# Layer 2 of a hybrid decoder step: when the evictions, reloads and the decode chain are issued

## The chip, the cores and the metric

One core of a Trainium2 chip runs the whole kernel. The metric is the device time of one execution in microseconds (us); the kernel before takes 1352.14 us (median of 3 runs, 1352.06 to 1353.18). The engines are PE (TensorE), DVE (VectorE), ACT (ScalarE) and POOL (GpSimd), each with its own queue of instructions that it works off in order; SP (SyncE) issues most transfers from a queue of its own.

## The reference, cut to what matters

Two layers run over a prompt of 1024 tokens and 8 single decode tokens, with model width 1024, in float32. Layer 1 is retention and is not touched. Layer 2 is sliding-window attention with 16 query heads of 64 in 2 groups and a window of 128:

```python
h = rmsnorm(x, g_norm)
q, k, v, gate = jnp.split(h @ w_in, [SWA_Q, SWA_Q + SWA_KV, SWA_Q + 2 * SWA_KV], axis=-1)
q, k = rmsnorm(q, q_gain), rmsnorm(k, k_gain)          # per head
# prompt: query block i of 128 reads key blocks i-1 and i
scores = q @ k.T * SWA_HD ** -0.5 - slope * dist        # banded, ALiBi
p = sink_softmax(scores, sinks)                         # one more column, dropped afterwards
o = (p @ v) * jax.nn.silu(gate)
return x + o @ w_out
# decode: the same over cache_k, cache_v (128 positions) and the new token
```

## The kernel before

Every operand of a big matmul is held as a high part and a low part, `A_hi` and `A_lo`, weights `wh` and `wl`. One product is three matmuls of 128 rows: high by high (L1134), high by low (L1135), low by high (L1136). `proj` writes these three for one k of eight.

Layer 2 begins near 900 us with keys and values. Then the q and gate projections run for 8 pairs of heads (`pair_proj`). A pair has three column groups of the tokens, `TG`: 0 to 384, 384 to 768, 768 to 1032 (the last 8 are the decode tokens), and so 6 tiles of 24 matmuls: q0, q1, q2, g0, g1, g2 (for the last pair g0 stands before q2 and g1 before g2). The tiles take turns on two PSUM banks (`pj`). A q tile is evicted by `q_hi` (ACT: a square for the norm, two high parts) and a tick later by `q_lo` (DVE: two low parts); a gate tile by `g_x` (DVE), `g_t` (ACT) and `g_m` (POOL, two products). `ms_mm` and `ms_ev` find the norm factors `rq`, with a power function on POOL (L118).

The attention has 64 units, one for a pair and a block of 128 tokens. A loop over frames m works on four units at once; in frame m it does `att_s` and `att_b` for unit m+3 (scores on PE, bias and maximum on DVE), `att_e` (exponentials, ACT) and `att_n` (DVE reciprocal, POOL multiplication, line L1680) for unit m+2, `att_x`, `att_ph`, `att_pl` (PE transposes into `tr`, ACT and DVE split) for unit m+1, `att_o` for unit m (product with the values into the single bank `o`, L1710 and L1708), and `att_c` for unit m-1 (two ACT copies at 0.5, two DVE operations L1732, one POOL product with the gate).

A frame has three thirds. Each ends with `work(0.865)`, which lets the projections put about 0.865 us of matmuls into the PE queue, and with `tick()`, which issues what `later(d, ...)` had put off by d ticks. Within layer 2's frames the order of the code is the order in each engine's queue, so a wait of one instruction holds all behind it on that engine.

Other work goes into the frames as jobs (`Job`, `loads`, `parts`). A job loads a raw tile `wr` (two buffers) and then runs its parts, at most two a frame. A part is the conversion of 512 columns of a weight (ACT high, POOL low, L1105 and L1106), a transposition of the key cache, or a reload of the gated attention output. That output is stored to DRAM (`oscr`) per pair and column group, since `A_hi` and `A_lo` still hold the gate's input. `reload_jobs(ti)` brings k = 0 to 6 of a column group back in four pieces, when all gate tiles of that group are done (`g7`): ACT writes `A_hi`, DVE writes `A_lo` (L1485). k = 7 comes straight from `att_st`.

When the projections are used up, `work` takes tiles of the output projection (`so_all`) instead. `start` runs 7 of 8 k-steps into a bank once the whole column group is reloaded (`rready`), `finish` does the last one, adds the residual on DVE (L1878) and has the tile before it transposed and stored (`so_y`). The column groups are gone through one after the other, six row tiles (`ft`) each, and tiles 6 and 7 at the end.

The decode tokens are a chain of five steps after the last frame: `dec_r` (a norm factor on DVE with a POOL power, L1754 to L1758), `dec_scores` (PE, L1770), `dec_soft` (DVE and ACT), `dec_pt` (PE transposes), `dec_o` (PE, L1812). Between them the tail does a reload part and fills PE with output tiles. At that point the order by hand ends (`sk.close()`), and the framework sets the order of all but PE.

Of the kernel before, what the change touches and what calls it, by code (L numbers as in the profile page):

```python
# [73 lines left out]
def _trunk(ctx, tc, nc, a):  # L74
# [1363 lines left out]
    rready = [False] * 3  # L1438

    class Job:  # L1440
        def __init__(self, load, parts, can_load=None, can=None):
            self.load, self.parts = load, list(parts)
            self.can_load, self.can, self.at = can_load, can, None

# [6 lines left out]
    def cache_job():  # L1451
        def load():
            kcT["c"] = wp.tile([128, 8, 128], F32, tag="wr", bufs=2, name="wr")
            nc.sync.dma_start(out=kcT["c"], in_=cache_k[0].rearrange("b s g d -> s b (g d)"))
            kcT["t"] = acc[:, 0:1024].rearrange("p (b s) -> p b s", b=8)

        def part(hf):
            pt = trp.tile([128, 512], F32, name="tr")
            for i in range(4):
                tr(pt[:, i * 128:i * 128 + 128], kcT["c"][:, 4 * hf + i, :], ident)  # L1460
            nc.scalar.activation(acc[:, 512 * hf:512 * hf + 512], pt, AF.Copy)

# [5 lines left out]
        jobs.append(Job(load, [lambda: part(0), lambda: part(1), new]))  # L1468

    def reload_jobs(ti):  # L1470

        t0, t1 = TG[ti]
        t1 = min(t1, NP)
        n = t1 - t0
        for k in range(0, 7, 2):
            m = min(2, 7 - k)
            g = {}

            def load(k=k, m=m, g=g):
                g["t"] = wp.tile([128, 2, n], F32, tag="wr", bufs=2, name="wr")  # L1480
                nc.sync.dma_start(out=g["t"][:, :m, :], in_=oscr[k:k + m, :, t0:t1].rearrange("k p t -> p k t"))

            def part(k=k, m=m, g=g):
                nc.scalar.activation(A_hi[:, k:k + m, t0:t1], g["t"][:, :m, :], AF.Copy)
                nc.vector.tensor_tensor(A_lo[:, k:k + m, t0:t1], g["t"][:, :m, :], A_hif[:, k:k + m, t0:t1],  # L1485
                                        ALU.subtract)
# [29 lines left out]
    def pair_proj(p):  # L1516
# [42 lines left out]
        def ms_ev(ti, pm):  # L1559
            t0, t1 = TG[ti]  # L1560
            nch = (min(t1, NP) - t0) // 128
            c0 = t0 // 128
            ee = e9[:, c0:c0 + nch].unsqueeze(2).broadcast_to([128, nch, 2])
            rq = atp.tile([128, 3, 2], F32, name="rq", bufs=4)
            rqn = rq[:, :nch, :]
            rqf = rq.rearrange("p c i -> p (c i)")[:, :2 * nch]

            nc.vector.scalar_tensor_tensor(rqn, pm[:, :2 * nch].rearrange("p (c i) -> p c i", i=2), 1.0 / HD, ee,
                                           ALU.mult, ALU.add)
            rsq(rqf, rqf, 2 * nch)  # L1570
            if ti == 2:
# [18 lines left out]
        def g_m(ti, gx, gt):  # L1590
            n = TG[ti][1] - TG[ti][0]
            nc.gpsimd.tensor_tensor(gt[:, :n], gt[:, :n], gx[:, :n], ALU.mult)  # L1592
# [6 lines left out]
        mms = {(1, 3): 0, (2, 3): 1, (4 if p == 7 else 3, 3): 2}  # L1599
        for step, (kind, ti) in enumerate(order):  # L1600
# [11 lines left out]
            for k in range(8):  # L1612
# [3 lines left out]
                if k == 7:  # L1616
                    (q_hi if isq else g_x)(ti, ps[:, :n])
# [22 lines left out]
    def bias_tab(h):  # L1640

        ndp[h] = atp.tile([128, 256], F32, name="ndp", bufs=3)
        nc.gpsimd.tensor_scalar(ndp[h], negd, SLOPE[h], None, ALU.mult)

# [106 lines left out]
    def dec_r():  # L1751
# [6 lines left out]
        nc.vector.tensor_tensor(r16, r16, rr, ALU.mult)  # L1758
        ddec = dd["ddec"] = atp.tile([16, 129], F32, tag="s", name="ddec", bufs=6)
        nc.sync.dma_start(out=ddec, in_=a["c2"][0:16, c2w() - 129:])  # L1760
        vc = dd["v"] = wp.tile([128, 8, 128], F32, tag="wr", bufs=2, name="wr")
# [17 lines left out]
    def dec_soft():  # L1779
        S16 = dd["S"]  # L1780
        nc.vector.tensor_tensor(S16, S16, dd["ddec"].unsqueeze(1).broadcast_to([16, 8, 129]), ALU.add)
        nc.vector.tensor_reduce(m16, S16, mybir.AxisListType.X, ALU.max)
        nc.vector.tensor_scalar(m16, m16, skc, None, ALU.max)
# [4 lines left out]
        nc.vector.tensor_reduce(t16, S16, mybir.AxisListType.X, ALU.add)  # L1788
        nc.vector.tensor_tensor(t16, t16, e16, ALU.add)
        nc.vector.reciprocal(t16, t16)  # L1790
        nc.vector.tensor_tensor(S16, S16, t16.unsqueeze(2).broadcast_to([16, 8, 129]), ALU.mult)
# [43 lines left out]
    def so_y(ft, ti, yt):  # L1835
        t0, t1 = TG[ti]
        npr = min(t1, NP) - t0
        nch = npr // 128
# [3 lines left out]
        if ti == 2:  # L1842
            tr(pt[:8, 256:384], yt[:, 256:264], ident)
        yo = atp.tile([128, 384], F32, tag="ot", name="yo", bufs=2)
# [7 lines left out]
    def so_all():  # L1852
        order = [(ft, ti) for ti in range(3) for ft in range(6)] + [(ft, ti) for ft in (6, 7) for ti in range(3)]
        early = []

        def start(ft, ti):
            t0, t1 = TG[ti]
            n = t1 - t0
            while so_slot(ft // 2) is None or not rready[ti] or (ti == 2 and "done" not in dd):
# [7 lines left out]
            for k in range(7):  # L1867
                proj(ps[:, :n], slot, ft % 2, t0, t1, first=(k == 0), last=False, ks=[k])
# [3 lines left out]
        def finish():  # L1872
# [4 lines left out]
            yt = io("sq", 2)  # L1877
            nc.vector.tensor_tensor(yt[:, :n], ps[:, :n], xr[:, :n], ALU.add)  # L1878
            if pend_y:
                so_y(*pend_y.pop(0))  # L1880
            pend_y.append((ft, ti, yt))
# [10 lines left out]
        while pend_y:  # L1892
            so_y(*pend_y.pop(0))
# [98 lines left out]
    for m in range(-L, NU + 1):  # L1992
        frame[0] = m
        w = W if m >= 0 else 1.15
        new, e, x, o, c = unit(m + L), unit(m + L - 1), unit(m + 1), unit(m), unit(m - 1)
# [14 lines left out]
        if e:  # L2010
            att_n(e)
        if x:
# [14 lines left out]
        parts(*((2, 1) if m >= 50 else (1, 2)))  # L2027
        loads()
        work(w)
        tick()  # L2030
    while post:
        tick()
    sk.close()
    steps = [dec_r, dec_scores, dec_soft, dec_pt, dec_o]
    while jobs or steps:
        frame[0] += 2
        loads()
        parts(1, 0)
        fill(out, 1.0)
        if steps and not (steps[0] is dec_r and len(jobs) > 1):  # L2040
            steps.pop(0)()
            fill(out, 1.5)
# [39 lines left out]
```

## Time and profile before

| | |
|---|---|
| median of 3 runs | 1352.14 us (1352.06 to 1353.18) |
| profiled execution | 1350.48 us, of which the span from first to last instruction is 1348.7 |
| PE busy, weight loads busy | 1300.1 us (96%), 1237.7 us (92%) |
| DVE, ACT, POOL busy | 746.6, 667.9, 819.9 us |
| PE busy from 900 us on | 426.2 of 448.7 us |
| mean granted clock of PE | 0.989 |

Busy times overlap, since the engines work side by side. PE is busy nearly always, so only two things can be gained around it: time in which it waits, and time in which its clock is below full. The profile names a waiting instruction by its line, and what released it. An idle engine other than PE costs nothing by itself.

### The profile page before, as it was taken

How to read it: one execution, taken by the hardware profiler on the slowest of the kernel's cores; microseconds unless marked ns; L12 is line 12 of the kernel's file. 1: busy time of each engine (PE TensorE's matmuls, PEld its weight loads, DVE VectorE, ACT ScalarE, POOL GpSimd, SP SyncE). 2: the span in 40 equal slices, each digit the busy share in tenths (PEclk: the TensorE clock that was granted, in tenths of full speed). 3: DMA queues.
4: the chain of work that ended last, by engine and by line, in shares of the span. 5: the costliest groups of instructions: out<-in, count | busy, mean ns of one | idle time of the engine just before them, and what ended most of it. 6: DMA issues, size and time to landing. Idle time of an engine off the chain costs nothing. (4 is left out here: it accounts for less than half of the span.)

```text
span 1348.7 us, 25969 instructions
## 1 busy us (share of the span) xinstructions
PE 1300.1 (96%) x9421; PEld 1237.7 (92%) x9421; DVE 746.6 (55%) x1507; ACT 667.9 (50%) x1692; POOL 819.9 (61%) x958
## 2 busy tenths in 40 slices
PE   6999999999999999899989999999999999997998
PEld 6999999999999999787877889999999999996998
DVE  6943655666565653577762212326777677776511
ACT  5532555555565653576750112245666767665321
POOL 6753555647556664598976663545778877766110
PEclk9999999999999999999998999999999999997999
DMA  6314767577676852656545444443022111013532
GB/s 221 104 55 134 224 200 239 164 236 227 185 227 196 242 159 69 209 177 211 165 164 176 142 154 135 129 117 98 23 63 64 42 48 42 23 53 112 156 89 80
DMA packets 193859, 187.18 MB, mean 139 GB/s; under 512 B 12756, under 2 KB 173580, under 8 KB 193716
## 3 DMA queue, kind: packets, MB, share of 16 engines
q1 hardware_dynamic: 160336, 153.19, 36.8%
q10 hardware_dynamic: 33396, 32.34, 7.7%
q8 instruction: 74, 1.21, 0.4%
q14 instruction: 53, 0.43, 0.1%
HBM read 129.11 MB, written 57.41 MB: 138 GB/s over the span
## 5 line engine op out<-in xcount | busy, mean ns | idle before, releaser
L340 PE MATMUL b<-xh,woh 128*128 128x258 f32 x784 | 222.2, 283 | 0.0
L342 PE MATMUL b<-xh,wol 128*128 128x258 f32 x784 | 221.7, 283 | 0.0
L341 PE MATMUL b<-xl,woh 128*128 128x258 f32 x784 | 221.4, 282 | 0.0
L1134 PE MATMUL pj<-A_hi,wh 128*128 128x384 f32 (+1 forms) x512 | 174.3, 340 | 0.0
L1135 PE MATMUL pj<-A_lo,wh 128*128 128x384 f32 (+1 forms) x512 | 165.6, 323 | 0.1
L1136 PE MATMUL pj<-A_hi,wl 128*128 128x384 f32 (+1 forms) x512 | 165.2, 323 | 0.0
L340 PEld LDWEIGHTS b<-xh,woh 128*128 128x128 f32 x784 | 148.1, 189 | 1.2
L341 PEld LDWEIGHTS b<-xl,woh 128*128 128x128 f32 x784 | 148.7, 190 | 0.0
L342 PEld LDWEIGHTS b<-xh,wol 128*128 128x128 f32 x784 | 148.0, 189 | 0.0
L1124 POOL TENSOR_TENSOR wl<-wr,wh 128x1024 fp32r<-128x1024 f32 (+1 forms) x40 | 88.5, 2222 | 87.4 <-ACT wh L1121 50.6
L334 PE MATMUL b<-wol,xh 128*128 128x256 f32 x448 | 126.0, 281 | 1.2 <-DVE wol L224 1.2
L333 PE MATMUL b<-woh,xh 128*128 128x256 f32 x448 | 125.8, 281 | 0.0
L335 PE MATMUL b<-woh,xl 128*128 128x256 f32 x448 | 125.7, 281 | 0.0
L282 POOL TENSOR_TENSOR yl<-yd,yh 128x256 fp32r<-128x256 f32 x64 | 56.4, 882 | 80.9 <-PE od L289 39.0
L1135 PEld LDWEIGHTS pj<-A_lo,wh 128*128 128x128 f32 x512 | 97.7, 191 | 0.4 <-DVE A_lo L1747 0.4
L224 POOL TENSOR_TENSOR wol<-raw,woh 128x512 fp32r<-128x512 f32 x52 | 68.8, 1331 | 48.1 <-ACT woh L219 47.2
L1134 PEld LDWEIGHTS pj<-A_hi,wh 128*128 128x128 f32 x512 | 97.5, 190 | 0.4
L1136 PEld LDWEIGHTS pj<-A_hi,wl 128*128 128x128 f32 x512 | 97.2, 190 | 0.0
L1680 POOL TENSOR_TENSOR s<-s,sm 128x512 f32<-128x512 f32 x64 | 66.4, 1038 | 31.9 <-DVE sm L1679 30.1
L334 PEld LDWEIGHTS b<-wol,xh 128*128 128x128 f32 x448 | 84.3, 188 | 1.4 <-DVE wol L224 1.4
L333 PEld LDWEIGHTS b<-woh,xh 128*128 128x128 f32 x448 | 84.3, 188 | 0.7
L335 PEld LDWEIGHTS b<-woh,xl 128*128 128x128 f32 x448 | 84.3, 188 | 0.0
(386 smaller groups left out, 3868.6 us busy)
## 6 DMA issues: line engine op xcount, KB each, us to landing
raw<-in_w_in_ret_dram ACTq DMA_DIRECT2D x44, 512.0 KB
st<-in_state_ret_dram SPq DMA_DIRECT2D x64, 256.0 KB
out_dram<-st SPq DMA_DIRECT2D x64, 256.0 KB
wr<-in_w_out_ret_dram SPq DMA_DIRECT2D x32, 512.0 KB
wr<-in_w_in_swa_dram SPq DMA_DIRECT2D x18, 512.0 KB
vb<-vscr SPq DMA_DIRECT2D x64, 128.0 KB
evp<-qks SPq DMA_DIRECT2D x32, 256.0 KB
evw<-gsc SPq DMA_DIRECT2D x32, 256.0 KB
```

The source lines that it names most:

```text
L224: eng.tensor_tensor(lo, src_of(s, name, sub), hi.bitcast(F32), SUB)
L333: mm(dst, xh, wh, start=a and i == 0, stop=False, skip_group_check=True)
L334: mm(dst, xh, wl, start=False, stop=False, skip_group_check=True)
L335: mm(dst, xl, wh, start=False, stop=z, skip_group_check=True)
L340: mm(dst, wh, xh, start=a, stop=False, **sg)
L341: mm(dst, wh, xl, start=False, stop=False, **sg)
L342: mm(dst, wl, xh, start=False, stop=z, **sg)
L1124: lo_eng[0].tensor_tensor(lo[:, js, :], raw[:, i:i + step, :], hi.bitcast(F32)[:, js, :], ALU.subtract)
L1134: mm(ps, hi[:, k, fs], xh[:, k, t0:t1], start=first and k == ks[0], stop=False)
L1135: mm(ps, hi[:, k, fs], xl[:, k, t0:t1], start=False, stop=False)
L1136: mm(ps, lo[:, k, fs], xh[:, k, t0:t1], start=False, stop=last and k == ks[-1])
L1680: nc.gpsimd.tensor_tensor(u.st[:, :, 0:256], u.st[:, :, 0:256], u.sm.unsqueeze(2).broadcast_to([128, 2, 256]), ALU.mult)
```

## The change

The frame is issued in another order: `att_n` stands right after `att_e`, `att_pl` after `att_ph`, and `att_c` moves from the next frame's start to the end of its own frame, behind the last `work` and ahead of the job parts. `q_hi` and `g_x` are put off by one tick, so that they no longer stand in the engines' queues before their tile is finished; `q_lo` follows another tick later. `ms_mm` moves from k-step 3 to 5.

A counter `spent` adds up what POOL gets beside the attention (`ms_ev` 1.35, `g_m` 2.05, `bias_tab` 0.85, a conversion 1.3, a reload piece 1.0 per k). Each frame takes 2.6 off it, and a part is put off while it would pass 3.4. Reload subtractions go to POOL, except two of the first column group. A piece may be loaded as soon as it is stored, and the output projection starts on the k-steps that are there (`rready` counts them). Its tiles go four row tiles at a time over the first two column groups. The adds, transposes and stores of a tile are put off by a tick each while the order is by hand. The decode chain is cut into eleven steps, of which the first two come in the last four frames, and the others one by one in a tail that is now also ordered by hand.

First place: DVE at the wait of PE for `ot` in the fourth pair (near 1041 us; `qs` is the q tile's low part, `ot` releases the bank `o`, `s` and `mx` are bias and maximum). Before:

```order
L1698 TENSOR_TENSOR ptl_13524<-tr_13515,pth_13520 128x512
L1542 SCALAR_TENSOR_TENSOR qs_13545<-pj_13470,gq_9853,qs_13545 64x384
L1544 SCALAR_TENSOR_TENSOR qs_13545<-pj_13470,gq_9853,qs_13545 64x384
L1732 SCALAR_TENSOR_TENSOR ot_13428<-o_13532,t0_13557 64x128
L1732 SCALAR_TENSOR_TENSOR ot_13428<-o_13532,ot_13428 64x128
L1668 SCALAR_TENSOR_TENSOR s_13537<-sc_13552,rq_13260,ndp_12940 128x256
```

and now:

```order
L1706 TENSOR_TENSOR ptl_13530<-tr_13523,pth_13528 128x512
L1740 SCALAR_TENSOR_TENSOR ot_13430<-o_13543,t0_13557 64x128
L1740 SCALAR_TENSOR_TENSOR ot_13430<-o_13543,ot_13430 64x128
L1547 SCALAR_TENSOR_TENSOR qs_13538<-pj_13459,gq_9853,qs_13538 64x384
L1549 SCALAR_TENSOR_TENSOR qs_13538<-pj_13459,gq_9853,qs_13538 64x384
L1676 SCALAR_TENSOR_TENSOR s_13548<-sc_13566,rq_13274,ndp_12961 128x256
```

The two `ot` operations have moved ahead of the two `qs`.

Second place: DVE at the last pair's first unit (near 1217 us; `r16` is the decode chain's first step, `A_lo<-wr` a reload, `sq<-pj` a gate tile, `sm` the reciprocal). Before:

```order
L1581 TENSOR_TENSOR sq_16009<-pj_15911,rbc_11599 128x384
L1679 RECIPROCAL sm_16000<-sm_16000 128x2
L1755 TENSOR_TENSOR r16_11575<-r16_11575,rbc_11599 16x8
L1756 TENSOR_SCALAR r16_11575<-r16_11575 16x8
L1758 TENSOR_TENSOR r16_11575<-r16_11575,rbc_11599 16x8
L1698 TENSOR_TENSOR ptl_16023<-tr_16014,pth_16019 128x512
L1485 TENSOR_TENSOR A_lo_7712<-wr_15976,A_hi_7711 128x2x384
L1485 TENSOR_TENSOR A_lo_7712<-wr_15980,A_hi_7711 128x384
L1732 SCALAR_TENSOR_TENSOR ot_16061<-o_16037,t0_16062 64x128
```

and now:

```order
L1587 TENSOR_TENSOR sq_16001<-pj_15905,rbc_11599 128x384
L1676 SCALAR_TENSOR_TENSOR s_15986<-sc_16004,rq_15797,ndp_15595 128x256
L1676 SCALAR_TENSOR_TENSOR s_15986<-sc_16004,rq_15797,ndp_15779 128x256
L1678 TENSOR_REDUCE mx_16009<-s_15986 128x2
L1687 RECIPROCAL sm_16013<-sm_16013 128x2
L1706 TENSOR_TENSOR ptl_16037<-tr_16030,pth_16035 128x512
L1740 SCALAR_TENSOR_TENSOR ot_16061<-o_16047,t0_16062 64x128
L1740 SCALAR_TENSOR_TENSOR ot_16061<-o_16047,ot_16061 64x128
L1489 TENSOR_TENSOR A_lo_7712<-wr_15863,A_hi_7711 128x384
```

The r chain is gone from here, and one reload of one k is left, behind `ot`.

Third place: POOL in the last pair's frames after the second column group's first units (`s` is the multiplication for a unit, `wl` a weight conversion, `ot` the gate product, `r16` the power function). Before:

```order
L1734 TENSOR_TENSOR ot_16258<-ot_16258,gt_16012 128x128
L1680 TENSOR_TENSOR s_16175<-s_16175,sm_16269 128x2x256
L1734 TENSOR_TENSOR ot_16258<-ot_16258,gt_16012 128x128
L1680 TENSOR_TENSOR s_16240<-s_16240,sm_16334 128x2x256
L1106 TENSOR_TENSOR wl_16363<-wr_16316,wh_16362 128x512 x2
L1734 TENSOR_TENSOR ot_16258<-ot_16258,gt_16012 128x128
```

and now:

```order
L1742 TENSOR_TENSOR ot_16252<-ot_16252,gt_16028 128x128
L1489 TENSOR_TENSOR A_lo_7712<-wr_16196,A_hi_7711 128x2x384
L118 TENSOR_TENSOR r16_11575<-r16_11575,mhalf_70 16x8
L1688 TENSOR_TENSOR s_16242<-s_16242,sm_16332 128x2x256
L1742 TENSOR_TENSOR ot_16252<-ot_16252,gt_16028 128x128
L1489 TENSOR_TENSOR A_lo_7712<-wr_16263,A_hi_7711 128x2x384
```

POOL now has the second group's reload pieces and the r chain's power here, and the weight conversion comes later. On PE, 54 projection matmuls stand between the decode scores and the decode transposes, where there were 42.

The diff, cut:

```diff
 def reload_jobs(ti):
+            eng = nc.vector if ti == 0 and k % 4 == 2 else nc.gpsimd
...
-                nc.vector.tensor_tensor(A_lo[:, k:k + m, t0:t1], g["t"][:, :m, :], A_hif[:, k:k + m, t0:t1],
+                eng.tensor_tensor(A_lo[:, k:k + m, t0:t1], g["t"][:, :m, :], A_hif[:, k:k + m, t0:t1],
                                         ALU.subtract)
-                if k == 6:
-                    rready[ti] = True
-            jobs.append(Job(load, [part], can_load=lambda: (6, ti) in stored and ti in g7))
+                rready[ti] = k + m
+            jobs.append(Job(load, [part], can_load=lambda k=k, m=m: (k + m - 1, ti) in stored,
+                            can=lambda: ti in g7, cost=1.0 * m if eng is nc.gpsimd else 0.1))
-    def parts(n, lead=2):
+    def parts(n, lead=2, limit=3.4):
...
-            if j.can is not None and not j.can():
+            if (j.can is not None and not j.can()) or spent[0] + j.cost > limit:
                 break
+            spent[0] += j.cost
...
-        mms = {(1, 3): 0, (2, 3): 1, (4 if p == 7 else 3, 3): 2}
+        mms = {(1, 5): 0, (2, 5): 1, (4 if p == 7 else 3, 5): 2}
...
-                    (q_hi if isq else g_x)(ti, ps[:, :n])
+                    later(1, q_hi if isq else g_x, ti, ps[:, :n])
...
-        order = [(ft, ti) for ti in range(3) for ft in range(6)] + [(ft, ti) for ft in (6, 7) for ti in range(3)]
+        order = [(ft, ti) for fs, ts in ((range(4), (0, 1)), ((4, 5), (0, 1)), (range(6), (2,)), ((6, 7), range(3)))
+                 for ti in ts for ft in fs]
...
             for k in range(7):
+                while rready[ti] <= k:
+                    yield 1e9
...
-            yt = io("sq", 2)
-            nc.vector.tensor_tensor(yt[:, :n], ps[:, :n], xr[:, :n], ALU.add)
...
+            soon(so_add, y)
...
-    for m in range(-L, NU + 1):
+    steps = [dec_r1, dec_r2, dec_d, dec_v, dec_scores, dec_s1, dec_s2, dec_s3, dec_s4, dec_pt, dec_o]
+    for m in range(-L, NU):
+        spent[0] = max(0.0, spent[0] - 2.6)
         if new:
             att_s(new)
-        if c:
-            att_c(c)
-        if new:
             att_b(new)
         if e:
             att_e(e)
+            att_n(e)
         work(w)
         tick()
         if x:
             att_x(x)
             att_ph(x)
-        if e:
-            att_n(e)
-        if x:
             att_pl(x)
...
-        parts(*((2, 1) if m >= 50 else (1, 2)))
+        work(w)
+        if o:
+            att_c(o)
+        parts(2, 1 if m >= 50 else 2)
         loads()
-        work(w)
+        if m >= NU - 4 and steps and steps[0] in (dec_r1, dec_r2) and (7, 2) in RQ:
+            steps.pop(0)()
         tick()
+    while steps or jobs:
+        frame[0] += 1
+        spent[0] = 0.0
+        loads()
+        parts(1, 1)
+        work(0.9)
+        if steps and not (steps[0] is dec_v and len(jobs) > 1):
+            steps.pop(0)()
+        work(0.9)
+        tick()
```

More of the change, by code (lines that the diff above doesn't have):

```diff
@@ L1437, in _trunk, with __init__ @@
     oready = [False] * 3
[L1438 removed]
+    rready = [0] * 3
     class Job:
[L1441 to L1442 removed]
+        def __init__(self, load, parts, can_load=None, can=None, cost=1.3):
+            self.load, self.parts, self.cost = load, list(parts), cost
             self.can_load, self.can, self.at = can_load, can, None
+    spent = [0.0]
     def weight_jobs(n):
@@ L1466, in new @@
             nc.scalar.activation(kdT, pt[:, 0:8], AF.Copy)
-        jobs.append(Job(load, [lambda: part(0), lambda: part(1), new]))
+        jobs.append(Job(load, [lambda: part(0), lambda: part(1), new], cost=0.2))
     def reload_jobs(ti):
@@ L2032, in _trunk @@
         tick()
+    ordered[0] = False
     sk.close()
[L2034 to L2042, printed above, removed]
     drain(out)
```

56 lines of the change are left out of this document (42 added, 14 removed).

## The prediction

> **What bounds the kernel now.** I read the busy times first, then the stage windows, then what TensorE (PE) waits for, then the rows around each long wait. The page's first part says that PE is the bound almost everywhere:
>
> ```profile
> PE 1300.1 (96%) x9421; PEld 1237.7 (92%) x9421; DVE 746.6 (55%) x1507; ACT 667.9 (50%) x1692; POOL 819.9 (61%) x958
> ```
>
> The diff touches layer 2 alone, which begins at about 900 us. The windows of that part (columns: window, length, busy time of PE, PEld, DVE, ACT, POOL, granted clock, DMA share, GB/s), and three short ones in which the clock was low:
>
> ```profile
> 945.00:1200.00 255.00, 248.95 (x1764) 242.60 (x1764) 187.21 (x474) 170.21 (x506) 200.71 (x283) 1.00 0.14 41
> 1200.00:1290.00 90.00, 78.24 (x492) 75.17 (x491) 52.38 (x109) 40.77 (x109) 35.93 (x44) 0.91 0.42 128
> 1290.00:1348.70 58.70, 54.85 (x390) 53.95 (x388) 7.36 (x15) 10.37 (x28) 5.08 (x4) 1.00 0.29 81
> ...
> 1221.00:1227.00 6.00, 6.00 (x23) 5.90 (x24) 4.02 (x10) 3.66 (x11) 4.41 (x9) 0.50 0.58 206
> 1240.80:1246.20 5.40, 5.37 (x26) 5.37 (x27) 3.22 (x7) 3.53 (x9) 1.04 (x1) 0.70 0.25 73
> 1284.90:1288.40 3.50, 3.50 (x13) 3.50 (x13) 0.64 (x3) 0.76 (x4) 0.00 (x0) 0.52 0.70 219
> ```
>
> PE idles 6.0 us in the steady frames, 11.8 us between 1200 and 1290, and 3.9 us at the end, which is the last eviction and store and stays. The low clock costs 6.0 x 0.50 = 3.0, 5.4 x 0.30 = 1.6 and 3.5 x 0.48 = 1.7 us, 6.3 us in all. The waits of PE after 900 us, whole list (waited for: us, times, longest):
>
> ```profile
> PE o L1710 <- DVE ot L1732: 6.1, 4, 3.7
> PE tr L103 <- DVE sq L1878: 5.7, 2, 5.4
> PE tr L103 <- POOL s L1680: 4.4, 9, 1.0
> PE tr L103 <- DVE rbc L1791: 1.4, 1, 1.4
> PE sc L1659 <- DVE qs L1542: 0.6, 1, 0.6
> PE sc L1659 <- DVE qs L1544: 0.2, 1, 0.2
> ```
>
> They sum to 18.4 us. So 18.4 + 6.3 = 24.7 us is all that this change can recover; the number of matmuls is the same.
>
> **The change part by part.** *Evictions a tick later, att_c at the frame's end.* The PE, ACT and DVE rows at one steady wait:
>
> ```profile
> 1041.24 0.47 PE L1710 MATMUL o<-pth,vv 128*128 128x256 f32 x2 [1.11 <-DVE ot L1732]
> ...
> 1038.69 0.58 ACT L1529 ACTIVATE qs<-pj,gq 64x384 fp32r<-64x384 f32 x1
> ...
> 1039.31 0.61 DVE L1542 SCALAR_TENSOR_TENSOR qs<-pj,gq,qs 64x384 fp32r<-64x384 f32 x1 [2.06 <-ACT qs L1529]
> 1039.93 0.62 DVE L1544 SCALAR_TENSOR_TENSOR qs<-pj,gq,qs 64x384 fp32r<-64x384 f32 x1
> 1040.47 0.29 DVE L1732 SCALAR_TENSOR_TENSOR ot<-o,t 64x128 f32<-64x128 f32 x1
> ```
>
> The one bank of `o` is released by the two `ot` operations, and DVE does the two q corrections (0.61 + 0.62 us) first. In the new order the `ot` pair stands ahead of them, so about 0.9 us of this 1.11 goes; ACT still copies q ahead, so 0.3 is left. Of the four waits (6.1 us), the longest has another cause:
>
> ```profile
> 1221.00 0.77 PE L1710 MATMUL o<-pth,vv 128*128 128x256 f32 x2 [3.65 <-DVE ot L1732]
> ...
> 1217.34 0.95 DVE L1758 TENSOR_TENSOR r<-r,rbc 16x8 f32<-16x8 f32 x1 [1.74 <-POOL r L118]
> 1218.21 0.67 DVE L1698 TENSOR_TENSOR ptl<-tr,pth 128x512 fp32r<-128x512 f32 x1
> 1218.81 1.41 DVE L1485 TENSOR_TENSOR A_lo<-wr,A_hi 128x768 fp32r<-128x768 f32 x2
> 1220.25 0.29 DVE L1732 SCALAR_TENSOR_TENSOR ot<-o,t 64x128 f32<-64x128 f32 x1
> ```
>
> DVE sat 1.74 us on GpSimd's power function, then did 1.41 us of reload, all ahead of `ot`. After the change the last step of that r chain is issued a frame later and one 384-column reload, behind `ot`, is left there: 3.65 goes, and with it the 3.0 us of half clock that follow it. The start's 0.8 us (`sc` waits for q) has two more k-steps, 6 matmuls, ahead of it; a matmul step is 0.17 us:
>
> ```profile
> 1289.03 0.34 PE L1136 MATMUL pj<-A_hi,wl 128*128 128x384 f32 x1
> 1289.20 0.34 PE L1134 MATMUL pj<-A_hi,wh 128*128 128x384 f32 x1
> ```
>
> That is 1.0 us of cover against 0.8; the later eviction takes some back, and I leave 0.3. Who waits for the later release of the projection's bank: the tile after next, a whole tile (24 x 0.17 = 4.1 us and the attention matmuls) away, against one tick of about a third of a frame; nothing.
>
> *The multiplication by 1/sum on GpSimd one third earlier; a budget.* Of the nine `tr <- s` waits, the largest, with GpSimd's groups:
>
> ```profile
> 1077.95 0.66 PE L103 MATMUL tr<-ident,s 128*128 128x128 f32 x4 [0.99 <-POOL s L1680]
> ...
> L1680 POOL TENSOR_TENSOR s<-s,sm 128x512 f32<-128x512 f32 x64 | 66.4, 1038 | 31.9 <-DVE sm L1679 30.1 <-DVE r L1755 1.8
> L1106 POOL TENSOR_TENSOR wl<-wr,wh 128x512 fp32r<-128x512 f32 x44 | 56.5, 1287 | 9.1 <-ACT wh L1105 8.7
> L118 POOL TENSOR_TENSOR r<-r,mhalf 16x8 f32<-16x8 f32 x1 | 1.6, 1626 | 0.1
> ...
> L1680 POOL TENSOR_TENSOR s<-s,sm x64: 1028/1037/1048, 946.1 to 1246.7; 128x512 f32<-128x512 f32 x64
> ```
>
> A frame is (1246.7 - 946.1) / 63 = 4.77 us, a third 1.6 us, more than any of the nine waits. But the total on GpSimd in the steady frames does not fall (200.7 of 255 us, 79%), and counted along the new order with these durations the heaviest stretch between two `s` is 6.3 us (6.0 before), so the budget does not level it. Bounds: 0 and, if nothing helps, 4.4; I leave 1.5, a third, since only the heavy frames can still be late.
>
> *Reloads.* Of twelve subtractions DVE keeps two; GpSimd gets five of 768 columns, three of 512, one of 384 and one of 256. By 1.29 us per 512 that is 5 x 1.9 + 3 x 1.29 + 1.0 + 0.65 = 15 us, upper value. They fall in 1200 to 1290, where GpSimd is idle for 54 of 90 us, so they cost only where PE stands behind one. The wait that they shall remove:
>
> ```profile
> 1240.83 0.90 PE L103 MATMUL tr<-ident,sq 128*128 128x128 f32 x3 [5.45 <-DVE sq L1878]
> ...
> 1237.01 0.96 DVE L1485 TENSOR_TENSOR A_lo<-wr,A_hi 128x768 fp32r<-128x768 f32 x1 [0.75 <-ACT A_hi L1484]
> ...
> 1236.13 0.84 ACT L1484 ACTIVATE A_hi<-wr 128x768 fp32r<-128x768 f32 x1 [1.32 <-DMA wr<-oscr]
> ...
> 1232.64 3.47 DMA wr<-oscr
> ```
>
> The output tile's add waits on DVE behind a reload that waits for its DMA. In the new order no DVE reload stands there: the 5.7 us go, and the 1.6 us of low clock behind them. What is late next is the reload of columns 384 to 768. Its last load (k = 6) needs the buffer that GpSimd frees with k = 2, 3. From the attention product of unit 61: `t`, `ot` and the gate about 1.6 us, GpSimd's `s` queue up to 1 us, the subtraction 1.9, the load 3.47, ACT's half-size copy about 0.5, GpSimd's last subtraction 1.0, together 8.5 to 9.5. PE's way to its use there is 39 matmuls x 0.17 = 6.6 us, two products (0.47 each) and two sets of transposes (under 0.66 each), about 8.5 us. So 0 to 1 us; several hops can slip, and I take 1.5 with bounds 0 and 5.5 (as now). On SP the loads also pass `xr` loads and wait in line for buffers; an `xr` behind one lands some 4 us before its transpose.
>
> *Decode chain in steps.* PE's one wait there:
>
> ```profile
> 1277.92 0.66 PE L103 MATMUL tr<-ident,rbc 16*128 16x16 f32 x9 [1.42 <-DVE rbc L1791]
> ```
>
> 54 matmuls instead of 42 now lie between the scores and these transposes, 12 x 0.17 = 2.0 us against 1.42. Bounds 0 and 1.4; I take 0.3.
>
> Two pages of the Trainium skill bear on it. The page SBUF — State Buffer, section "Who interferes with whom", has GpSimd and a DVE operation with two SBUF inputs exclude each other for a whole instruction. The row at 1217.34 agrees (0.95 us for 16x8 elements). By that rule the decode softmax could meet the last 256-column reload, 0.65 us, and the 0.3 would be 1.0. The page TensorE: Matmul & The Clock Gate, section "What's actually happening", ties the half clock to an idle window of about 3.4 us. After 3.65 and 5.45 us of waiting the trace agrees (0.50, 0.70). The stretch from 1284.9 contradicts it: clock 0.52 with PE busy throughout. By the rule its 1.7 us could go with the 1.42 us wait, and the forecast would be 1331.3.
>
> I go by the row: the small decode matmuls just ahead stay, so the 1.7 us stay.
>
> *Sum.* Left over: 0.3 (start) + 0.3 (`o`) + 1.5 (`s`) + 1.5 (reload) + 0.3 (decode) + 1.7 (clock) = 5.6. Recovered: 24.7 - 5.6 = 19.1 us. The profiled execution, 1350.48 us (span 1348.7 and 1.8 around it), becomes 1331.4. The median of the runs shown, 1352.14, is 1.7 above it: **1333**.
>
> **The rivals.** (1) *A new long wait in the tail.* For it: the reload chain above is serial, and ACT stands still for the k = 6 load with the next weights behind it. Against it: the slack elsewhere there is microseconds. If that wait is 4 us instead of 1.5, a half-clock stretch like the 3.0 follows: 1333 + 2.5 + 3.0 = 1338.5. (2) *Steady frames keep their 6.0 us*, since GpSimd now waits for the reciprocal at its queue's head with the same total: 1333 + 6.0 - 1.8 (the 0.3 and 1.5 left above) = 1337. (3) *GpSimd becomes the bound, slower.* 54 steady frames (255 / 4.77) have 54 us of GpSimd idle. If `s` in its earlier place makes GpSimd wait 1.0 us more per frame, the idle is used up; every further 0.1 us costs 5.4. From 1.36 us on the 19.1 are lost, and at 1.45 it is 1333 + 24 = 1357. For it: GpSimd already waits 31.9 / 64 = 0.5 us ahead of each `s`. Against it: the exponentials it waits for keep their place. (4) *The later evictions hold the two projection banks*: a wait of 0.4 us in each of 48 tiles eats the gain, 1352; for it only that the bank is freed up to two ticks later.
>
> **How the numbers follow.** Forecast 0.62 (its own range 1328 to 1337), rival 1 0.14, rival 2 0.12, rival 3 0.07, rival 4 0.05. The range goes from 1327.4 = 1352.1 - 24.7, everything recovered, to 1342: rival 1 with the reload's upper bound is 1333 + 4.0 + 3.0 = 1340, and half of rival 2's 4 us beside it. A measurement of this kernel can tell about 0.2% from no change. Faster by more 0.88, within 0.05, slower 0.07.
>
> **What would show it.** Right: the waits of PE for `ot` and for the output tile's `sq` fall below 1 us each; no low-clock window near 1220 and 1240; `s` waits fewer than nine; GpSimd's busy time up by some 13 us and DVE's down by some 8, at 1200 to 1290. Wrong: a PE wait for A_lo over 3 us with a clock near 0.5 behind it, or 945 to 1200 us without its gain. The forecast fails if a wait that has cover now (q's banks, weights late by the budget) loses it.

## The result, and the profile after

The changed kernel takes 1337.37 us (median of 4 runs, 1335.32 to 1338.05) against 1352.1 of before: ratio 0.9883, 95% interval 0.987 to 0.9897. The forecast was 1333, range 1327.4 to 1342, so the sign and the range held and the point was 4.4 us too low. The profiled execution took 1338.05 us, its span is 1336.3. The first part of its page:

```profile
PE 1293.8 (97%) x9421; PEld 1233.6 (92%) x9421; DVE 743.8 (56%) x1497; ACT 668.4 (50%) x1692; POOL 832.5 (62%) x968
```

The stages of layer 2 in the profile after, and the one stretch in which the clock was low (window, length, busy time of PE, PEld, DVE, ACT, POOL, granted clock, DMA share, GB/s):

```profile
945.00:1200.00 255.00, 250.48 (x1794) 246.75 (x1793) 189.81 (x479) 176.35 (x518) 202.59 (x286) 1.00 0.15 44
1200.00:1290.00 90.00, 84.89 (x557) 81.29 (x556) 50.71 (x100) 39.64 (x108) 46.34 (x51) 0.98 0.43 131
1290.00:1336.30 46.30, 41.79 (x305) 40.96 (x303) 5.69 (x12) 8.91 (x25) 5.08 (x4) 0.99 0.29 80
1276.00:1280.60 4.60, 4.60 (x22) 4.60 (x22) 1.11 (x4) 1.26 (x5) 0.00 (x0) 0.63 0.51 136
```

All waits of PE after 900 us in the profile after (waited for: us, times, longest):

```profile
PE tr L103 <- POOL s L1688: 5.4, 7, 1.4
PE tr L103 <- DVE sq L1869: 2.0, 3, 1.1
PE tr L103 <- DVE rbc L1813: 1.4, 1, 1.4
PE pj L1135 <- POOL A_lo L1489: 0.7, 1, 0.7
PE pj L1135 <- DVE A_lo L1755: 0.3, 1, 0.3
```

The reader is to see three things. The waits are 9.8 us instead of 18.4; the low clock costs 4.6 x 0.37 = 1.7 us instead of 6.3, since the two long waits that had a half-clock stretch behind them (3.65 and 5.45 us) are gone. (The third such stretch, 1.7 us near the decode step, is there in both profiles.) PE's idle time falls from 6.0 to 4.5 us in the steady frames, and from 11.8 to 5.1 us between 1200 and 1290. So most of the gain is in the last frames: 6.7 us of idle and 4.6 us of low clock there, 2.3 us ahead of 1200 (the start's 0.8 included), less 0.7 us of a longer end. That is 12.9 us against 1350.48 - 1338.05 = 12.4 measured. And the largest remainder, the wait for `s`, has not shrunk at all: 5.4 us against 4.4.

### The profile page after: what moved, and what is told of

Its sections match the earlier page's. It is cut to its first block, busy times and chain, and to the rows that moved or that the text cites. A ratio compares the mean times of both kernels' runs of the same rounds, so it can differ in the third digit from the quotient of the medians.

```text
span 1336.3 us, 25984 instructions
## 1 busy us (share of the span) xinstructions
PE 1293.8 (97%) x9421; PEld 1233.6 (92%) x9421; DVE 743.8 (56%) x1497; ACT 668.4 (50%) x1692; POOL 832.5 (62%) x968
## 5 line engine op out<-in xcount | busy, mean ns | idle before, releaser
L224 POOL TENSOR_TENSOR wol<-raw,woh 128x512 fp32r<-128x512 f32 x52 | 68.9, 1333 | 48.0 <-ACT woh L219 47.0
```

What stands on the lines that cost most here:

```text
L224: eng.tensor_tensor(lo, src_of(s, name, sub), hi.bitcast(F32), SUB)
```

## The experiments

Each ratio is to the kernel before, run beside it on the same chip. A label with b_ is built on the kernel before, one with a_ on the kernel after.

| kernel | median us | ratio | 95% interval |
|---|---|---|---|
| after | 1337.37 | 0.9883 | 0.987 to 0.9897 |
| b_pin | 1350.81 | 0.999 | 0.9981 to 0.9998 |
| b_out | 1345.02 | 0.9952 | 0.994 to 0.9964 |
| b_outpin | 1342.84 | 0.9934 | 0.9919 to 0.9949 |
| b_attn | 1355.62 | 1.0026 | 1.0017 to 1.0035 |
| b_reload | 1352.78 | 1.0002 | 0.9992 to 1.0012 |
| a_attn | 1336.82 | 0.9888 | 0.9872 to 0.9904 |
| a_dve | 1337.16 | 0.9888 | 0.9873 to 0.9903 |
| a_nolimit | 1353.04 | 1.0006 | 0.9997 to 1.0015 |
| a_order | 1343.77 | 0.994 | 0.9925 to 0.9955 |
| a_parts1 | 1335.07 | 0.9877 | 0.9858 to 0.9896 |
| a_attn_p1 | 1336.19 | 0.9892 | 0.9874 to 0.991 |
| a_p1_pf | 1331.85 | 0.9848 | 0.9835 to 0.9861 |

### One part alone, on the kernel before

**b_pin: the r chain in the hand-written order.**

```diff
+    dec_r()            # without its two loads, which stay a step behind
     sk.close()
-    steps = [dec_r, dec_scores, dec_soft, dec_pt, dec_o]
+    steps = [dec_l, dec_scores, dec_soft, dec_pt, dec_o]
```

> The kernel before, with one part of the change: the r chain of the decode step (r <- ms, r; five small operations on VectorE and one on GpSimd) is issued inside the hand-written order behind the last frame, instead of behind its end, from where it had risen ahead of the `ot` operations at 1217. Theory (each wait is its own, and the gain is their sum): the 3.65 us wait of PE for `ot` falls to 1 us or less, the 3.0 us lost to half clock behind it go, all else stays: 1352.1 - 2.7 - 3.0 = 1346.5. Rival (the reload subtractions on VectorE ahead of `ot`, 1.41 us, make the wait and the chain only rides along): the wait stays over 2 us, the clock window at 1221 stays near 0.5: 1350 to 1351. Rival 2 (the lost time is handed on): the chain now stands ahead of the output tile's add, so the 5.45 us wait for `sq` grows by some 3 us: no gain, 1352.

PE's wait for `ot` fell from 3.65 to 2.08 us. VectorE's rows ahead of that wait in b_pin:

```profile
1214.40 2.44 DVE L1485 TENSOR_TENSOR A_lo<-wr,A_hi 128x768 fp32r<-128x768 f32 x2
1216.87 0.29 DVE L1732 SCALAR_TENSOR_TENSOR ot<-o,t 64x128 f32<-64x128 f32 x1
```

Two reloads, 2.44 us, now stand directly ahead of `ot`, and the result lies at the rival's 1350 to 1351. The chain's removal is worth 1.6 us of that wait. The other way round, with the chain left in place and the 768-column reload gone from VectorE (b_reload, below), 3.19 us of it stay. So taking one away is not enough, and the two shares do not add up to the whole.

**b_out: the order of evictions.**

```diff
-        if c:
-            att_c(c)           # at the start of the next frame
...
         work(w)
+        if o:
+            att_c(o)           # at the end of its own frame
...
-                    (q_hi if isq else g_x)(ti, ps[:, :n])
+                    later(1, q_hi if isq else g_x, ti, ps[:, :n])
...
-        mms = {(1, 3): 0, (2, 3): 1, (4 if p == 7 else 3, 3): 2}
+        mms = {(1, 5): 0, (2, 5): 1, (4 if p == 7 else 3, 5): 2}
```

> The kernel before, with the new order of evictions alone: the projection's evictions one tick later (their mean-square matmuls two k-steps later), and the eviction of the attention product at the end of its own frame. Theory: the three short waits for `ot` (6.1 - 3.65 = 2.4 us) and the two for q at the start (0.8 us) go; the long wait for `ot` keeps some of its length unless the new place lets `ot` pass the r chain: 1352.1 - 3.2 = 1349, or 1342.5 if the long wait and its 3.0 us of low clock go too. Rival (later evictions hold the two projection banks): new waits of the projection matmuls for qs or sq, 0.4 us in each of 48 tiles: 1352 or more.

The measured 7.2 us lies between the theory's two values and is the largest of any part alone. Its steady frames and all its waits of PE after 900 us:

```profile
945.00:1200.00 255.00, 253.69 (x1821) 250.29 (x1819) 192.92 (x481) 180.10 (x529) 204.62 (x289) 1.00 0.15 45
```

```profile
PE tr L103 <- POOL s L1680: 6.5, 7, 4.0
PE pj L1134 <- ACT A_hi L1746: 3.2, 1, 3.2
PE o L1710 <- DVE ot L1732: 2.9, 2, 2.3
PE tr L103 <- DVE rbc L1791: 1.4, 1, 1.4
PE tr L103 <- DVE sq L1878: 0.3, 1, 0.3
```

In the steady frames PE is busy for 253.69 us, 4.7 more than before and 3.2 more than in the whole change. No wait of the projection for its banks appears: that rival falls. The 5.45 us wait for `sq` is gone too, with every reload still on VectorE. But in the last frames its place is taken by waits of 4.0 us (`s`, behind 3.44 us in which VectorE stands at the r chain's GpSimd step), 3.2 (A_hi) and 2.3 us (`ot`). So this part alone is worth more than the whole change in the steady frames, and part of it is handed on in the last ones. The rows ahead of the 3.2 us wait show where it comes from:

```profile
1226.12 0.84 ACT L1484 ACTIVATE A_hi<-wr 128x768 fp32r<-128x768 f32 x1 [5.28 <-DMA wr<-oscr]
...
1229.15 0.52 ACT L1746 ACTIVATE A_hi<-ot 128x384 fp32r<-128x384 f32 x1 [1.73 <-POOL ot L1734]
```

ScalarE stood 5.28 us at a reload copy for its load; the two copies of `o`, VectorE's `ot` pair, GpSimd's gate product and the A_hi that PE waits for follow one another behind it.

**b_outpin: both together.**

> The kernel before with two parts of the change together, the new order of evictions and the r chain issued behind the last frame in the hand-written order. The first alone gave 1345.0 and left a wait of 4.0 us for `s` at 1218, behind VectorE's 3.4 us wait for the chain's GpSimd step, the second alone 1350.8. Theory (the chain is what ate the first one's gain): the 4.0 us wait and about 2 us of low clock behind it go, 1345.0 - 6 = 1339. Rival (the 3.2 us wait for A_hi at 1230 has its own cause in the reloads and takes over with its low clock): 1342 to 1345.

1342.84: the rival. In the profile, of an execution of 1345.62 us, the longest wait for `s` fell from 4.0 to 1.9 us and a second of that length came; the wait for A_hi was still there (3.7 us, again behind a reload copy, which waited 5.24 us for its load), and the clock stood at 0.50 from 1228 to 1234. The interval overlaps with that of b_out. Two parts do not make the change; 5.5 us are missing.

**b_attn: the multiplication a third of a frame earlier.**

```diff
             att_e(e)
+            att_n(e)
         work(w)
...
-        if e:
-            att_n(e)
```

> The kernel before, with the reciprocal and GpSimd's multiplication s <- s, sm issued one third of a frame earlier, and nothing else. Theory as forecast: the nine waits of PE for `s` (4.4 us) fall to a third, 1.5 us: 1349. Rival A (the place in the frame does not matter, since the work that GpSimd does between two `s` sets when the next is done): `s` waits stay at 4 us or more, 1352. Rival B (GpSimd stands at its queue's head for the exponentials and its 54 us of idle are used up): `s` waits of over 10 us, 1357 or more.

It made the kernel slower, 1.0026, between rival A's 1352 and rival B's 1357. PE's waits for `s` in the steady frames rose from 3.9 to 6.0 us, and VectorE shows a path to it. Its waits for GpSimd's small copy (`s`, L1649) ahead of the maximum, in the steady frames of before and of b_attn:

```profile
DVE mx L1670 <- POOL s L1649: 2.0, 8, 0.4
```

```profile
DVE mx L1670 <- POOL s L1649: 8.7, 8, 1.5
```

The earlier multiplication waits at the head of GpSimd's queue (GpSimd's idle time ahead of `s` in the steady frames goes from 23.8 to 33.1 us), so the copy of the sink column behind it comes late; the maximum of a later unit waits for the copy, then its exponentials, then the next `s`. After has the same wait, 8.8 us. It is not the only path: ahead of the longest wait, 1.31 us at 1157.21, GpSimd had worked without a pause since 1148.93. No run takes the two apart on the kernel before.

**b_reload: the subtractions on GpSimd.**

```diff
+            eng = nc.vector if ti == 0 and k % 4 == 2 else nc.gpsimd
...
-                nc.vector.tensor_tensor(A_lo[...], g["t"][...], A_hif[...], ALU.subtract)
+                eng.tensor_tensor(A_lo[...], g["t"][...], A_hif[...], ALU.subtract)
```

> The kernel before, with the reload subtractions moved from VectorE to GpSimd (all but two), and nothing else. Theory: the add of the output tile no longer stands behind a reload on VectorE, so of the waits for `sq` (5.7 us) over 4 go, and the 1.6 us of low clock behind them; the long wait for `ot` loses at most the 1.4 us of the reload ahead of it: 1352.1 - 4.5 - 1.6 - 1 = 1345. Rival (the wait comes from the load's landing and is only handed on): a wait of PE for A_lo of 4 us or more in its place, low clock behind it: 1352. Rival 2 (GpSimd's gate product for `ot` and the multiplication of `s` queue behind the reloads): new waits for `s` above 2 us in the last frames: 1350.

No effect, 1.0002, and the wait that it should have removed is there. VectorE's and ScalarE's rows ahead of it in b_reload:

```profile
1239.92 0.29 DVE L1734 SCALAR_TENSOR_TENSOR ot<-o,t 64x128 f32<-64x128 f32 x1 [2.65 <-ACT ot L1732]
...
1241.55 0.69 DVE L1672 TENSOR_REDUCE mx<-s 128x2 f32<-128x514 f32 x1
1242.16 1.01 DVE L1880 TENSOR_TENSOR sq<-pj,xr 128x384 f32<-128x384 f32 x2
...
1238.59 0.84 ACT L1486 ACTIVATE A_hi<-wr 128x768 fp32r<-128x768 f32 x1 [1.35 <-DMA wr<-oscr]
1239.46 0.27 ACT L1732 ACTIVATE t<-o 64x128 f32<-64x128 f32 x1
```

PE waited 4.96 us for that `sq`. No reload stands on VectorE there any more; the add now queues behind the `ot` pair, which waits 2.65 us for ScalarE. ScalarE makes the copies for that pair behind its own half of the reload, which waited 1.35 us for its load. So the wait for the load is handed on, as the rival had it, though by way of ScalarE and `ot` and not to A_lo. The new order of evictions takes the wait for `sq` away (b_out, 0.3 us left).

### One part undone, on the kernel after

**a_attn: the multiplication back in the second third** (the lines of b_attn, reversed).

> The kernel after with one part undone: the reciprocal and GpSimd's multiplication of `s` go back to the second third of the frame, between the copies pth and ptl. Theory: in its earlier place the multiplication holds GpSimd's queue for the exponentials, so GpSimd's copy of the sink column behind it comes late, VectorE's maximum waits for that copy (8.8 us in the steady frames of after, 2.9 us with the order of evictions alone), and the next `s` is late. Undone, the waits for `s` between 945 and 1200 fall from 4.5 to about 1.3 us, and the maximum's wait to about 3: 1337.4 - 3.2 = 1334. Rival A (the budget's two weight conversions in one frame make these waits): they stay at 4 us or more, 1337. Rival B (the earlier place pays in the last frames, where GpSimd does the reloads): waits for `s` after 1200 of over 2 us, 1339 or more.

1336.82, not told apart from after. `s` in the steady frames fell from 4.5 to 3.9 us only, and the maximum's wait from 8.8 to 4.9: rival A, the conversions, is what remains.

**a_dve: all reloads on VectorE.**

```diff
-            eng = nc.vector if ti == 0 and k % 4 == 2 else nc.gpsimd
+            eng = nc.vector
```

> The kernel after with one part undone: all reload subtractions on VectorE again. Moving them alone, on the kernel before, brought nothing (ratio 1.0002). Theory: with the r chain in its place and the evictions in the new order VectorE has room, so what is undone costs little: waits after 1200 us within 2 us of after's 4.4, 1337 to 1339. Rival (the gain needs both: with reloads on VectorE the output tile's add is late again): a wait for `sq` of over 3 us with a clock under 0.8 behind it, 1342 to 1344.

1337.16, as the theory had it, with 1.4 us of waits for `sq`; its waits for `s` are longer (7.8 us), it has none for the decode softmax and no low clock. With b_reload this says from both sides that the engine of the reloads carries none of the gain that the times can show.

**a_nolimit: without the budget.**

```diff
-    def parts(n, lead=2, limit=3.4):
+    def parts(n, lead=2, limit=1e9):
```

> The kernel after without the budget: the limit of 3.4 us on GpSimd's other work in a frame is lifted, so two weight conversions go out in any frame in which they are ready. Theory: the budget levels little, since it counts the gate products only after the conversions of the frame are issued; waits for `s` after 900 us go from 5.4 to 6 to 8 us, time 1338 to 1340. Rival (the budget is what keeps the waits small, and after would be bound by GpSimd without it): waits for `s` of over 10 us, 1343 or more. Rival 2 (the budget itself pushes conversions into heavy frames): waits fall to 4 us or less, 1335.

The rival holds, and beyond its size: 1353.04, the whole gain lost. PE's waits for `s` after 900 us, and a part of GpSimd's rows in a_nolimit:

```profile
PE tr L103 <- POOL s L1688: 16.9, 12, 2.5
```

```profile
1147.13 2.55 POOL L1106 TENSOR_TENSOR wl<-wr,wh 128x512 fp32r<-128x512 f32 x2
1149.64 0.74 POOL L1599 TENSOR_TENSOR gt<-gt,sq 128x264 f32<-128x264 f32 x1
1150.46 0.74 POOL L1600 TENSOR_TENSOR gt<-gt,sq 128x264 f32<-128x264 f32 x1
1151.30 0.24 POOL L1602 TENSOR_SCALAR gdec<-gt 128x8 f32<-128x8 f32 x1
1151.50 1.04 POOL L1688 TENSOR_TENSOR s<-s,sm 128x512 f32<-128x512 f32 x1
```

Two conversions and two gate products stand ahead of the `s` at 1151.50, which PE waits 2.35 us for; two more conversions follow it from 1153.03 on. With the budget one conversion stands in that stretch. The clock fell to 0.50 behind the wait, and again at 1240. Of the 16.9 us, 9.0 lie after 1200, where not only conversions but reload pieces too go out two in a frame (3.62 us of GpSimd at 1231.21).

**a_order: the output tiles in the old order.**

```diff
-        order = [... for fs, ts in ((range(4), (0, 1)), ((4, 5), (0, 1)), (range(6), (2,)), ((6, 7), range(3))) ...]
+        order = [(ft, ti) for ti in range(3) for ft in range(6)] + [(ft, ti) for ft in (6, 7) for ti in range(3)]
```

> The kernel after with the output tiles in the order of before (all six feature tiles of columns 0 to 384, then all six of 384 to 768, then the rest). Theory: the four tiles of columns 384 to 768 that the new order brings forward are what PE does while the reloads and the last attention units of the first columns come in; without them a wait for A_hi or A_lo of about 3.5 us returns, as in the kernel before with the new evictions (3.2 and 3.7 us), with about 2 us of low clock: 1342 to 1343. Rival (the budget and the evictions one tick later have taken that wait's cause away): waits after 1200 within 1 us of after's 4.4, 1337.

The size was as the theory had it (1343.77, 6.4 us above after), the place was not. PE's longest wait in a_order:

```profile
PE pj L1134 <- ACT wh L1105: 6.0, 1, 6.0
```

PE waits for the next output weights: ScalarE's conversion stood 3.85 us for their load, which needs a buffer that GpSimd frees after the reloads. In after ScalarE stands there as well, 3.49 us ahead of 1246.97, and PE does not wait. In the old order the tiles that need these weights come before the tiles of columns 384 to 768. The new order is thus a part of the change in its own right, to which the prediction gave no term.

### Further on

**a_parts1: one conversion in a frame.**

```diff
-        parts(2, 1 if m >= 50 else 2)
+        parts(2 if m >= 50 else 1, 1 if m >= 50 else 2)
```

> The kernel after with one edit: at most one weight conversion issued in a frame before unit 50. The multiplication of `s` stays in its new, earlier place. Theory: with single conversions the place of the multiplication matters less than its load: `s` between 945 and 1200 falls from 4.5 to 2 us or less, 1337.4 - 2.5 = 1335. Rival (the earlier place costs by itself, since the sink copy behind it is late; on the kernel before it made 6.0 us out of 3.9): `s` stays at 3.5 to 6 us there, 1337 to 1339.

**a_attn_p1: the same, and the multiplication back.**

> The kernel after with two edits: the multiplication of `s` back in the second third of the frame, and at most one weight conversion issued in a frame before unit 50 (two before, if the budget allowed). Theory (two conversions in one frame, 2.55 us on GpSimd, make the steady waits for `s`; the kernel before and the new order of evictions alone issue one and wait 1.3 us there): `s` between 945 and 1200 falls from 3.9 us with the multiplication's place undone alone to about 1.3, PE's busy time there from 251.0 to about 253.5: 1336.8 - 2.6 = 1334. Rival (weights converted one at a time come later and projections wait for them, or the waits come from the place at the end of the frame where the conversions now stand): `s` stays near 4 us or new waits appear: 1337 or more.

The steady frames of a_parts1, and its waits for `s` after 900 us:

```profile
945.00:1200.00 255.00, 252.60 (x1809) 248.89 (x1808) 192.26 (x479) 178.35 (x525) 203.66 (x286) 1.00 0.15 44
```

```profile
PE tr L103 <- POOL s L1688: 3.3, 6, 1.0
```

PE gains 2.1 us of busy time there; the times alone (1335.07 and 1336.19) do not tell either kernel from after. In the steady frames the wait for `s` falls from 4.5 to 2.3 us in a_parts1 (2 or less was expected) and from 3.9 to 2.1 in a_attn_p1 (1.3 was expected). So two conversions in a frame make about half of it; why more is left than the 1.3 us of b_out, no run took apart. With single conversions the place of the multiplication is worth nothing that shows, 252.83 us busy with it back, 252.60 without, although it cost something on the kernel before. What the rows show ahead of such a wait is GpSimd busy without a pause.

**a_p1_pf: the residuals one tile ahead.** In after, one decode wait of 1.4 us was left. VectorE's rows ahead of it in the profile after:

```profile
1254.64 0.56 DVE L1869 TENSOR_TENSOR sq<-pm,xr 128x384 f32<-128x384 f32 x1 [4.79 <-DMA xr<-xscr]
1259.05 0.56 DVE L1869 TENSOR_TENSOR sq<-pj,xr 128x384 f32<-128x384 f32 x1 [3.85 <-DMA xr<-xscr]
1259.53 1.27 DVE L1785 TENSOR_TENSOR rbc<-sc,r 16x512 f32<-16x512 f32 x2
```

PE's decode scores ran from 1257.37 on (1.93 us), but VectorE stood at an output tile's add for `xr`, whose load waited on SP behind reload loads that wait for GpSimd's buffers.

```diff
-            xr = iop2.tile([128, 384], F32, tag="xr", bufs=2, name="xr2")
-            nc.sync.dma_start(out=xr[:, :n], in_=xscr[ft, :, t0:t1])
+            for nx in order[len(xrs):order.index((ft, ti)) + 2]:
+                xrs.append(atp.tile([128, 2, 384], F32R, name="qs", bufs=4).bitcast(F32)[:, 0, :])
+                a0, a1 = TG[nx[1]]
+                nc.sync.dma_start(out=xrs[-1][:, :a1 - a0], in_=xscr[nx[0], :, a0:a1])
+            xr = xrs[order.index((ft, ti))]
```

> The kernel after with single conversions before unit 50 and, besides, the residual of each output tile loaded one tile ahead (into the four buffers of qs, free by then), so that its load stands ahead of the reload loads on SP that wait for buffers. Theory (VectorE stands at the output tile's add for a residual that was issued behind such a load, and the decode scores' evictions queue behind that add): the add's waits for xr (4.8 and 3.9 us in after) fall below 1.5 us, PE's wait for the decode softmax (1.1 to 1.4 us) and the longest for `sq` (1.2 us) go: 1335.1 - 2 = 1333. Rival A (the adds then wait for the reloads' A_lo by way of PE, and the chain behind is as late): the xr waits go, PE's waits after 1200 stay within 0.5 us of 5: 1335. Rival B (the earlier residual loads now push the reload loads back on SP): a wait for A_lo of 2 us or more, 1337 or more.

All waits of PE after 900 us in a_p1_pf:

```profile
PE tr L103 <- POOL s L1688: 3.2, 5, 1.0
PE tr L103 <- DVE sq L1869: 1.4, 2, 1.2
PE pj L1135 <- POOL A_lo L1489: 0.7, 1, 0.7
PE pj L1135 <- DVE A_lo L1755: 0.3, 1, 0.3
```

The waits for `xr` and the decode wait are gone; the 1.2 us for `sq` stayed, so that one has another cause. 1331.85 us, ratio 0.9848 (0.9835 to 0.9861), whose interval lies below after's: this version beats both kernels. Against a_parts1 the intervals overlap; PE's waits between 1200 and 1290 are 3.1 us there against 5.0.

## Why the prediction was right or wrong, point by point

- **What can be recovered, 24.7 us**: the frame held. 24.7 less the 9.8 of waits and the 1.7 of low clock left, less 0.7 at the end, is 12.5; measured 12.4.
- **The sum**: of 5.6 us expected to be left, 11.5 are: `s` 3.9 more, reload 1.5, decode 1.1, start and `o` 0.6 less. With 0.7 us of a longer end that is the 6.6 us by which the profiled execution, 1338.05, missed the 1331.4. The medians differ by 4.4 only, since before's profiled execution was faster than its median and after's was slower.
- **Start 0.3 and `o` 0.3**: both 0. The order of evictions does it for the start and for the waits in the steady frames; b_out shows it alone.
- **The 3.65 us for `ot` and its 3.0 us of clock**: gone. The two causes named (chain and reload) both stand in the rows; without the chain 2.08 us stay (b_pin), without the larger reload 3.19 (b_reload).
- **`s`, 1.5: the step that failed; it measured 5.4**, above even the bound of 4.4 that was to hold if nothing helped. I read an earlier place in the frame as cover. b_attn and a_attn show that it is none: on the kernel before it raised the steady waits from 3.9 to 6.0 us, on the kernel after its undoing lowered them from 4.5 to 3.9. In a queue worked in order, an instruction moved ahead that must still wait keeps back what stands behind it. The larger share in after is the loop that offers two conversions a frame: 2.2 of the 4.5 us go with it (a_parts1). That the budget does not level GpSimd's load was half right: with it the two conversions still cost 2.1 us of PE's time, but without it the new loop loses everything (a_nolimit). I had counted the heaviest stretch, 6.3 us against 6.0, and then not used it. The steady wait at 1000.93 comes out of such a stretch in the profile after:

```profile
1000.93 0.66 PE L103 MATMUL tr<-ident,s 128*128 128x128 f32 x4 [1.36 <-POOL s L1688]
```

```profile
995.27 2.55 POOL L1106 TENSOR_TENSOR wl<-wr,wh 128x512 fp32r<-128x512 f32 x2
997.75 1.04 POOL L1599 TENSOR_TENSOR gt<-gt,sq 128x384 f32<-128x384 f32 x1
998.87 1.01 POOL L1600 TENSOR_TENSOR gt<-gt,sq 128x384 f32<-128x384 f32 x1
999.85 1.03 POOL L1688 TENSOR_TENSOR s<-s,sm 128x512 f32<-128x512 f32 x1
```

- **Reload, 1.5: measured 3.0**, and the reason was wrong. The waits for A_lo are 1.0 us, at the end of the 0 to 1 that the chain of loads gave, but 2.0 us for `sq`, the longest 1.15, stayed where all were to go. I put the end of the 5.45 us wait down to the engine of the reloads. b_reload keeps the wait without a reload on VectorE there, b_out loses it with all reloads in place. The forecast of GpSimd's busy time, +13, was right over the whole profile (+12.6; +10.4 between 1200 and 1290); VectorE's fell by 2.8 only, not 8.
- **Decode, 0.3: measured 1.4.** 54 matmuls of cover were there, but the scores' evictions began late for a residual. The prediction saw that residual loads stand in line with the reload loads on SP, and gave it no price.
- **Clock, 1.7: measured 1.7, in part by luck.** In a_p1_pf the decode wait is gone and the low clock is not, and in b_out the wait is there (1.4 us), the same small matmuls behind it, and no low clock:

```profile
1272.00:1274.00 2.00, 2.00 (x9) 2.00 (x8) 1.11 (x4) 0.94 (x4) 0.00 (x0) 0.62 0.57 177
1274.00:1276.00 2.00, 2.00 (x8) 2.00 (x8) 0.00 (x0) 0.00 (x0) 0.00 (x0) 0.53 0.87 251
```

```profile
1276.70:1283.20 6.50, 6.50 (x45) 6.46 (x45) 1.21 (x4) 1.26 (x5) 0.00 (x0) 1.00 0.44 124
```

  The reason given, that the small decode matmuls stay, does not carry it. Of the 14 profiles, seven have the low clock behind these 16 matmuls of 128x16 (before, after, b_outpin, a_attn, a_parts1, a_attn_p1, a_p1_pf) and seven do not; b_out, b_attn and b_reload keep before's decode chain and its wait of 1.4 us, and run on at 1.00. What decides it stays open. By the rule of the Trainium skill's page TensorE: Matmul & The Clock Gate, section "What's actually happening", the 1.7 us could have gone with the wait; a_p1_pf shows them without it. The same page calls the window free-running; no run here shows a window.
- **Rivals**: rival 1's long wait did not come in after, where no wait is over 1.4 us; its mechanism, the next weights behind the last reload load, is the 6.0 us wait of a_order. Of rival 2's steady 6.0 us, 4.5 stayed, in part for the reason it named. Rivals 3 and 4 did not come; rival 3's mechanism is b_attn, 1.0026.

My theory by then was a sum of separate waits. The parts alone fall by 1.4 and 7.2, rise by 3.4 and 0.6 us: together 4.6, against 14.7 for the whole. The budget and the order of tiles, 15.7 and 6.4 us when undone, are conditions for the rest. What stays open: which part removes the 3.2 to 3.7 us wait for A_hi of b_out and b_outpin. The reload pieces loaded as soon as they are stored, the output projection begun on the k-steps that are there, the later adds and the tail ordered by hand were never run apart.

## What to carry to other kernels

Moving a waiting instruction earlier on an engine that works its queue in order is not cover and can cost what stands behind it; count the work between two of the instructions that the bound engine waits for. Price a part by undoing it as well as by doing it alone: here the parts with the largest effect when undone (a limit on side work, the order of output tiles) had no price of their own in the forecast. A late load can stand behind another that waits for a buffer, so look at the order of its queue and load a tile ahead.

## What the runs showed of the hardware

A tiny VectorE operation ran for as long as GpSimd had work beside it. VectorE's and GpSimd's rows of the profile after:

```profile
1236.19 3.04 DVE L1768 TENSOR_TENSOR r<-r,rbc 16x8 f32<-16x8 f32 x1
```

```profile
1235.97 1.03 POOL L1688 TENSOR_TENSOR s<-s,sm 128x512 f32<-128x512 f32 x1
1236.96 0.45 POOL L1742 TENSOR_TENSOR ot<-ot,gt 128x128 f32<-128x128 f32 x1
1237.38 1.83 POOL L1489 TENSOR_TENSOR A_lo<-wr,A_hi 128x768 fp32r<-128x768 f32 x1
```

The 16x8 product took 3.04 us and ended as the third GpSimd instruction ended; in b_pin the same product took 0.155 us (at 1264.5), with GpSimd idle. The Trainium skill's page SBUF — State Buffer, section "Who interferes with whom", has such pairs exclude each other for a whole instruction; here it was three in a row. And the clock near 0.5 behind the small decode matmuls is not fixed to them: in a_dve, too, the same instructions (16 matmuls of 128x16, the first at 1269.45) ran on at 1.00, with PE busy throughout, as it is in the rows of a_p1_pf above.

```profile
1269.40:1276.00 6.60, 6.60 (x46) 6.51 (x45) 1.12 (x4) 1.26 (x5) 0.00 (x0) 1.00 0.46 134
```
